# Neighbourhood attention beside a projection stream: value products of two steps in one visit, and three items of the recurrent branch moved in the written order

## The chip, the core and the metric

One core of a Trainium2 chip runs the whole layer. The metric is the device time of the program in microseconds, the median of several executions. TensorE (PE) does the matrix products, VectorE (DVE) and ScalarE (ACT) the elementwise work, GpSimd (POOL) some multiplies and memsets, and SyncE (SP) issues most of the DMAs. Each engine works through its own queue in order and waits for the others at semaphores.

## The reference, cut to what matters

The program is one layer of a hybrid model: 512 latent tokens on an 8 x 64 grid and 128 context tokens, 1024 features. One branch is a recurrent one (RWKV-7, two directions), the other an attention over a neighbourhood of the grid:

```python
def row_block(args):
    q_r, r0, dr = args
    k_r = lax.dynamic_slice_in_dim(kg, r0, kr, axis=1)[:, :, k_col]
    v_r = lax.dynamic_slice_in_dim(vg, r0, kr, axis=1)[:, :, k_col]
    ...
    lw = jnp.einsum("bjqhd,bkjchd->bhjqkc", q_r, k_r).astype(jnp.float32) * scale + bias[None]
    lw = jnp.where(valid[:, :, None, :], lw, NEG_INF)
    lc = jnp.einsum("bjqhd,blhd->bhjql", q_r, k_ctx).astype(jnp.float32) * scale
    logits = jnp.concatenate([lw.reshape(bsz, h, n_cb, NA_QCOLS, n_win), lc], axis=-1)
    p = jax.nn.softmax(logits, axis=-1).astype(v.dtype)
    ...
    return (jnp.einsum("bhjqkc,bkjchd->bjqhd", pw, v_r)
            + jnp.einsum("bhjql,blhd->bjqhd", pc, v_ctx))
```

Context tokens attend to all context tokens. Of the recurrent branch only the preparation matters here: per direction a decay that is summed along the sequence in blocks of 64, and the keys, normalised per head (`kk = kk * rsqrt(sum(kk * kk))`) and scaled by the decay.

## The kernel before

The grid is cut into four blocks of 16 columns, 128 queries each; the context tokens are a fifth block. Eight heads are four pairs (`ft`). So there are twenty items `k = 5 * ft + j`, with `j` from 0 to 3 for the column blocks and 4 for the context. The value of an item passes through these functions:

- `na_l(k)`: logits of the two heads into one PSUM tile `lg` (L942). For `j < 4` VectorE adds the mask and bias and takes the maximum (L948), for `j = 4` it only reduces (L955). It returns the exponentials, which ScalarE does (L952 or L957).
- `na_m(k)`: VectorE's reciprocals of the sums (L964), then GpSimd's multiply of the weights, one per head (L965).
- `na_t(k)`: TensorE transposes the weights (L971) into two PSUM tiles `pt`, ScalarE copies them to `PT` (L976).
- `na_o(k)`: TensorE multiplies with the values (L989) into one PSUM tile `po`, twelve matmuls for `j < 4`: two chunks of the window and one of the context, for two heads. `split` then writes the rounded part into `on` (ScalarE, L204) and the rest (VectorE, L205). At `j = 4` the two tiles `on` of the head pair are sent to memory (`o_d`, L996). `on` has one buffer of each kind, so the next head pair's first split waits until these have been sent.

These are not called item by item but in 22 steps, written out by hand in the table `na`. Step `k` does `na_o(k - 2)`, `na_l(k)`, `na_t(k - 1)`, the exponentials of `k`, then `a` units of the projection stream (`some(a)`: matmuls of L216 into tiles `mm`, with the elementwise work that falls due), `na_m(k)`, `p` items of the recurrent branch's preparation, `b` more units of the stream, `q` more items, and `n` pieces of the modulation product (`ada`, matmuls of L1027 into `psa`, whose weights arrive in tiles `wa` and `f`). A table entry is `a.p.b.q.n`. In this stretch the order of TensorE, VectorE, ScalarE and GpSimd is the written one.

The preparation is a generator, `prep_0`, and `next(pre0)` is one item. Counted in its order, items 9 and 10 are the five transposes of the key norm into the two `pt` tiles (L671) and the product that reads them and makes `kk` (L674, L676, VectorE). Items 11 and 12 are scale and scan of the first direction (L685, L688), 19 and 20 those of the second. Items 24 to 27 are four products of the first direction on VectorE (L710, L715, L721, L725). In the table before, 9 and 10 are at the end of step 13, 19 and 20 behind `na_m(17)`, 26 and 27 behind `na_m(19)`. After the 22 steps comes the recurrent scan, which begins with VectorE's products into `AG` (L1148).

## Time and profile before

| | us |
|---|---|
| median of 3 executions | 1171.59 (1171.57 to 1172.24) |
| profiled execution | 1170.39 |
| its span, first to last instruction | 1168.6 |
| TensorE busy in it | 1123.1 |
| VectorE busy | 775.6 |
| ScalarE busy | 535.4 |
| GpSimd busy | 194.3 |

The profile is of one execution; its span is a little shorter than the time of the execution, and that execution is a little shorter than the median. Busy time of TensorE counts its matmuls from start to modelled end, so a TensorE that is busy throughout is not at its peak. In the rows below, the first two numbers are start and length in us from the span's start, the count stands behind the x, and the brackets hold the idle time of the engine before the row and what ended it. The attention steps run from 121 to 256 us.

### The profile page before, as it was taken

The numbers are of one execution on the slowest core, as the hardware profiler recorded it, in microseconds if no ns is written. First come the engines' busy times: TensorE is split into PE (matmuls) and PEld (weight loads), VectorE is DVE, ScalarE is ACT, GpSimd is POOL, SyncE is SP. The second block draws the span as 40 slices with busy tenths as digits, with TensorE's granted clock in tenths as the row PEclk, the third lists the DMA queues.
The fourth block names the chain that finished last, engine by engine and source line by source line (L and its number), as shares of the span: only waits on it lengthen the run. The fifth ranks groups of instructions, "written<-read, shape, count | busy, mean of one in ns | idle before, by whom it ended". The sixth has DMA issues, their size and how long they took to land.

```text
span 1168.6 us, 26884 instructions
## 1 busy us (share of the span) xinstructions
PE 1123.1 (96%) x11160; PEld 995.0 (85%) x11160; DVE 775.6 (66%) x1639; ACT 535.4 (46%) x1054; POOL 194.3 (17%) x264
## 2 busy tenths in 40 slices
PE   6999999999999999999899899989999999999998
PEld 4688877789888988888788778989899989998997
DVE  4565365569558847945577856877567756875775
ACT  4444566554565665557353424644224423441330
POOL 1163244320101212110200241100000000001000
PEclk9999999999999999999999999999999999999999
DMA  9752777654433433343843772322212321232122
GB/s 338 259 117 81 229 245 226 200 145 117 110 85 88 133 82 91 105 107 91 276 130 108 239 217 67 96 73 85 97 54 91 100 87 67 73 108 90 54 83 98
DMA packets 60770, 150.21 MB, mean 129 GB/s; under 512 B 7492, under 2 KB 22468, under 8 KB 60648
## 3 DMA queue, kind: packets, MB, share of 16 engines
q1 hardware_dynamic: 55464, 131.56, 34.4%
q0 software_dynamic: 4320, 15.73, 6.9%
q8 instruction: 88, 1.44, 0.5%
q10 hardware_dynamic: 864, 1.20, 0.4%
q14 instruction: 34, 0.28, 0.1%
HBM read 118.41 MB, written 14.32 MB: 114 GB/s over the span
## 4 chain that ended last, share of the span: by engine, by line
PE 60%; DVE 7%; issue 7%; ACT 3%; DMA 1%; SPq 0%; POOL 0%; DVEq 0%; ACTq 0%; POOLq 0%
PE f L1814 23%; PE acc L303 16%; PE fl L216 10%; DVE pr L1293 1%; PE mm L216 1%; PE w L1394 1%; DVE RL L1297 1%; PE w L1367 1%; PE w L1191 1%; PE w L1407 1%; DMA o<-o_d 1%; PE w L1379 1%; PE w L1169 1%; ACT wlo L183 1%; PE w L1239 0%
## 5 line engine op out<-in xcount | busy, mean ns | idle before, releaser
L1814 PE MATMUL f<-t,whi 128*128 128x320 f32 x640 | 141.4, 309 | 0.0
L1814 PE MATMUL f<-b,whi 128*128 128x320 f32 x608 | 136.4, 312 | 3.6 <-ACT b L204 1.8
L303 PE MATMUL acc<-whi,u 128*128 128x512 f32 (+1 forms) x448 | 135.9, 385 | 0.0
L216 PE MATMUL fl<-h,whi 128*128 128x320 f32 x672 | 121.3, 320 | 0.8 <-issue 0.8
L1814 PEld LDWEIGHTS f<-t,whi 128*128 128x128 f32 x640 | 106.9, 188 | 0.0
L1814 PEld LDWEIGHTS f<-b,whi 128*128 128x128 f32 x608 | 102.7, 189 | 4.7 <-ACT b L204 2.2
L216 PEld LDWEIGHTS fl<-h,whi 128*128 128x128 f32 x672 | 101.5, 188 | 5.5 <-issue 0.9
L185 ACT CAST whi<-wst 128x1024 fp32r<-128x1024 f32 (+1 forms) x77 | 79.1, 1033 | 56.1 <-PE acc L303 42.5
L1814 PE MATMUL f<-t,wlo 128*128 128x320 f32 x320 | 98.9, 309 | 0.0
L303 PEld LDWEIGHTS acc<-whi,u 128*128 128x128 f32 x448 | 83.5, 188 | 16.6
L1814 PE MATMUL f<-b,wlo 128*128 128x320 f32 x304 | 94.6, 311 | 1.4 <-DVE wlo L1858 1.4
L1855 ACT CAST whi<-ws 128x1024 fp32r<-128x1024 f32 x40 | 42.0, 1050 | 108.4 <-PE f L1814 48.2
L303 PE MATMUL acc<-wlo,u 128*128 128x512 f32 (+1 forms) x224 | 86.3, 385 | 0.0
L1869 POOL TENSOR_TENSOR ws<-wst 128x512 f32<-128x512 f32 x20 | 28.0, 1402 | 341.3 <-DVE wlo L1858 247.7
L188 DVE TENSOR_TENSOR wlo<-wst,whi 128x1024 fp32r<-128x1024 f32 (+2 forms) x55 | 58.3, 1072 | 31.8 <-ACT whi L185 31.2
L303 PE MATMUL acc<-whi,h 128*128 128x512 f32 x240 | 78.5, 401 | 0.8 <-DVE h L428 0.8
L1691 DVE SCALAR_TENSOR_TENSOR tt<-acc,G 128x512 f32<-128x512 f32 (+1 forms) x51 | 34.7, 680 | 59.3 <-PE acc L303 45.3
L216 PE MATMUL fl<-h,wlo 128*128 128x320 f32 x336 | 63.5, 321 | 0.0
L1855 ACT CAST whi<-wst 128x1024 fp32r<-128x1024 f32 (+1 forms) x48 | 41.3, 868 | 42.3 <-PE acc L303 25.1
L1814 PEld LDWEIGHTS f<-t,wlo 128*128 128x128 f32 x320 | 60.1, 188 | 0.0
L1858 DVE TENSOR_TENSOR wlo<-ws,whi 128x1024 fp32r<-128x1024 f32 x40 | 55.0, 1374 | 6.3 <-ACT whi L1855 6.3
L1814 PEld LDWEIGHTS f<-b,wlo 128*128 128x128 f32 x304 | 57.6, 190 | 1.7 <-DVE wlo L1858 1.7
(342 smaller groups left out, 2512.8 us busy)
## 6 DMA issues: line engine op xcount, KB each, us to landing
wst<-in_w_dram SPq DMA_DIRECT2D x66, 512.0 KB
wst<-in_w_rw_dram SPq DMA_DIRECT2D x31, 512.0 KB
wlo<-wst POOLq DMA_DIRECT2D x30, 512.0 KB, 4.6
wa<-in_w_ada_dram SPq DMA_DIRECT2D x24, 512.0 KB
f<-in_w_ada_dram SPq DMA_DIRECT2D x16, 512.0 KB
wst<-in_w_qkv_dram SPq DMA_DIRECT2D x12, 512.0 KB
o<-o_d SPq DMA_DIRECT2D x14, 320.0 KB
x<-in_xs_dram SPq DMA_DIRECT2D x8, 512.0 KB
```

What stands on the lines that cost most here:

```text
L183: act.activation(lo[:, :n], st[:, :n], AF.Copy, scale=-1.0)
L185: act.copy(hi[:, :n], st[:, :n])
L188: dve.tensor_tensor(out=lo[:, a:b], in0=st[:, a:b], in1=hi[:, a:b].bitcast(F32), op=ALU.subtract)
L216: pe.matmul(ps[:, :t1 - t0], w[:, a:a + 128], x[:, k0 + kt, t0:t1], start=n == 0, stop=n == 3 * nk - 1)
L303: pe.matmul(pss[i][:, a:b], lhs(x, kt, ts_), w[:, cs_], start=ki == 0 and n == 0, stop=ki == last and n == 2)
L1169: pe.matmul(t[r0:r0 + 32, 64 * i:64 * i + 64], S.BK[l // 10][own, l % 10, 0, 32 * bk:32 * bk + 32], V(AG[own, l, h, :], [[0, 2], [1, 32]], ...
L1191: pe.matmul(pr[h][hrows[h ^ i], o_], x[hrows[h], :], R_[hrows[h], l, :], start=True, stop=True)
L1691: dve.scalar_tensor_tensor(out=tt, in0=ps[:, a:b], scalar=c, in1=G[:, g, sl], op0=ALU.mult, op1=ALU.mult)
L1814: pe.matmul(ps[:, :H2], w_[:, c_], x_[:, kt, :], start=first and kt + n == 0, stop=last and kt == 3 and n == 2, skip_group_check=more)
L1855: act.copy(r[0][:, :width], src())
L1858: dve.tensor_tensor(out=r[1][:, :width], in0=src(), in1=r[0][:, :width].bitcast(F32), op=ALU.subtract)
L1869: eng_x(PRM["se"][i - 1]).tensor_tensor(out=o_, in0=x, in1=y, op=op)
```

## The change

`na_o` takes a count. Items 0 and 1 of a head pair are multiplied in one visit (two sets of twelve matmuls, into columns 0 to 127 and 128 to 255 of one `po` tile), items 2 and 3 in another, item 4 alone; one split serves both items of a visit. The visits of the four head pairs are in steps 3, 5 and 6, 8, 10 and 11, 13, 15 and 16, 18, 20 and 21; steps 2, 4, 7, 9, 12, 14, 17 and 19 have none. Before, each of the steps 2 to 21 has one. The table entry gains a sixth number: items of the preparation that come before `na_m(k)`. With it and the old numbers, items 9 and 10 go from the end of step 13 to behind `na_m(14)`, items 19 and 20 from behind `na_m(17)` to ahead of it, and items 26 and 27 from behind `na_m(19)` to ahead of it.

```diff
-        "6.0.12.0.2 6.0.12.1.0 6.1.12.1.2 6.2.12.2.0 6.1.12.2.2 6.0.12.2.0 6.1.12.1.2 6.2.14.2.0 "
-        "6.2.14.1.2 6.2.14.2.0 6.2.14.2.0 6.3.18.2.0 10.0.10.0.0"))
+        "6.0.12.1.0 6.1.12.1.2 6.2.12.2.0 6.1.12.0.2 6.2.12.2.0 6.1.12.1.2 6.2.14.2.0 6.0.14.1.2.2 6.2.14.2.0 "
+        "6.0.14.2.0.2 6.3.18.2.0 10.0.10.0.0"))
...
-            def na_o(k):
+            def na_o(k, nb):
...
-                vts = (*vch[j], cvt) if j < 4 else (vpr,)
-                for c, vt in enumerate(vts):
-                    for hd in range(2):
-                        hc = (2 * ft + hd) * 64
-                        pe.matmul(pso[64 * hd:64 * hd + 64, :128], vt[:, hc:hc + 64],
-                                  blk[k][hd][:, c * 128:(c + 1) * 128], start=c == 0, stop=c == len(vts) - 1)
+                for i in range(nb):
+                    vts = (*vch[j + i], cvt) if j < 4 else (vpr,)
+                    for c, vt in enumerate(vts):
+                        for hd in range(2):
+                            hc = (2 * ft + hd) * 64
+                            pe.matmul(pso[64 * hd:64 * hd + 64, 128 * i:128 * i + 128], vt[:, hc:hc + 64],
+                                      blk[k + i][hd][:, c * 128:(c + 1) * 128], start=c == 0, stop=c == len(vts) - 1)
                 if j < 4:
-                    split(*(V(t[:, :], [[1, 16], [64, 8]], 16 * j) for t in on[ft]), V(pso[:, :], [[8, 16], [1, 8]]))
+                    split(*(V(t[:, :], [[16, 2], [1, 16], [64, 8]], 16 * j) for t in on[ft]),
+                          V(pso[:, :], [[128, 2], [8, 16], [1, 8]]))
...
-                    a, p, b, q, n = (int(x) for x in step.split("."))
-                    if 2 <= k < 22:
-                        na_o(k - 2)
+                    a, p, b, q, n, s_ = (int(x) for x in (step + ".0").split(".")[:6])
+                    ft, j = divmod(k - 3, 5)
+                    if ft < 0 or ft > 3:
+                        pass
+                    elif j == 0:
+                        na_o(5 * ft, 2)
+                    elif j == 2:
+                        na_o(5 * ft + 2, 2)
+                    elif j == 3:
+                        na_o(5 * ft + 4, 1)
...
                     some(a)
+                    for _ in range(s_):
+                        next(pre0, None)
                     if k < 20:
                         na_m(k)
```

More of the change, by code (lines that the diff above doesn't have):

```diff
@@ L74 @@
     wl="dddddddddppppppppppppppppppppppppppdddd", nu=9, lg=14, jo=(2, 0, 1), na=(
-        "6.0.12.0.1 6.0.12.0.0 6.0.12.0.0 6.0.12.0.2 6.0.12.0.0 6.0.12.0.2 6.0.12.0.0 6.0.12.0.2 6.0.12.0.0 "
-        "6.0.12.0.2 6.0.12.1.0 6.1.12.1.2 6.2.12.2.0 6.1.12.2.2 6.0.12.2.0 6.1.12.1.2 6.2.14.2.0 "
-        "6.2.14.1.2 6.2.14.2.0 6.2.14.2.0 6.3.18.2.0 10.0.10.0.0"))
+        "6.0.12.0.1 6.0.12.0.0 6.0.12.0.0 6.0.12.0.2 6.0.12.0.0 6.0.12.0.2 6.0.12.0.0 6.0.12.0.2 6.0.12.0.0 6.0.12.0.2 "
+        "6.0.12.1.0 6.1.12.1.2 6.2.12.2.0 6.1.12.0.2 6.2.12.2.0 6.1.12.1.2 6.2.14.2.0 6.0.14.1.2.2 6.2.14.2.0 "
+        "6.0.14.2.0.2 6.3.18.2.0 10.0.10.0.0"))
 MANUAL = {mybir.EngineType.PE}
```

## The prediction, made before the change was run

> **What bounds the kernel now.** I read the page first, then the table of stretches, then the rows of each engine in time order through the attention stage (121 to 256 us). From the page one line carries the argument: the chain that ended last is mostly TensorE's own work.

> ```profile
> PE 60%; DVE 7%; issue 7%; ACT 3%; DMA 1%; SPq 0%; POOL 0%; DVEq 0%; ACTq 0%; POOLq 0%
> ```

> So an edit that leaves TensorE's work alone can gain only what TensorE waits, or runs at a reduced clock. The table of stretches (time, then busy time of TensorE and its weight loads, VectorE, ScalarE, GpSimd, granted clock, DMA) shows where this stage loses both:

> ```profile
> 220.00:240.00 20.00, 18.00 (x141) 15.01 (x139) 11.17 (x26) 13.36 (x34) 6.96 (x8) 0.91 0.39 128
> ```

> Two microseconds idle and a clock of 0.91. TensorE's rows in order of time (start, length, count, and in brackets the idle time before and what ended it) give the places:

> ```profile
> 206.84 0.85 PE L971 MATMUL pt<-K,L 128*128 128x128 f32 x6 [0.97 <-DVE kk L674]
> ...
> 210.25 0.66 PE L989 MATMUL po<-PT,va 128*64 128x128 f32 x8
> 210.74 0.39 PE L989 MATMUL po<-PT,cvt 128*64 128x128 f32 x4
> 211.06 0.70 PE L942 MATMUL lg<-bv,q 64*128 64x256 f32 x4
> ...
> 232.45 0.55 PE L971 MATMUL pt<-K,L 128*128 128x128 f32 x3 [0.57 <-POOL L L965]
> 234.42 0.55 PE L971 MATMUL pt<-K,L 128*128 128x128 f32 x3 [1.42 <-POOL P L692]
> 234.72 2.26 PE L216 MATMUL mm<-h,wlo 128*128 128x320 f32 x8
> 236.78 2.65 PE L216 MATMUL mm<-h,whi 128*128 128x320 f32 x12
> ...
> 246.12 0.33 PE L971 MATMUL pt<-K,L 128*128 128x128 f32 x1 [0.61 <-POOL L L965]
> 246.21 1.42 PE L216 MATMUL mm<-h,whi 128*128 128x320 f32 x8
> 247.47 1.34 PE L216 MATMUL mm<-h,wlo 128*128 128x320 f32 x8
> ```

> Each wait is of the transposes of the softmax weights (L971). In step 14 (206.84) they want the two `pt` tiles that the key product L674 still reads. In step 18 (232.45, 234.42) and step 20 (246.12) they want GpSimd's multiply L965; the memset L692 named at 234.42 only stands behind that multiply in GpSimd's queue. After step 18's waits the clock is halved: eight matmuls take 2.26 against 1.34 at 247.47, and twelve take 2.65, where 1.97 would be due (eight of them last from 246.21 to 247.47, 0.16 each, so four more add 0.63 to 1.34). The loss is 0.92 + 0.68 = 1.6 us.

> What is behind step 18's wait is read from the rows of ScalarE, VectorE and GpSimd:

> ```profile
> 225.84 0.39 ACT L204 CAST on<-po 128x128 fp32r<-128x128 f32 x1 [2.18 <-DMA o_d<-on]
> ```

> ```profile
> 209.74 1.57 DVE L688 TENSOR_TENSOR_SCAN pre<-K,pre 128x640 f32<-128x640 f32 x1
> ...
> 226.94 0.55 DVE L948 CUSTOM_DVE_ANT_1 L<-lg,bm 128x384 f32<-128x384 f32 x1
> ...
> 231.11 0.22 DVE L964 RECIPROCAL m<-m 128x1 f32<-128x1 f32 x2
> 231.24 0.47 DVE L685 TENSOR_SCALAR pre<-pre 128x640 f32<-128x640 f32 x1
> 231.75 1.99 DVE L688 TENSOR_TENSOR_SCAN pre<-K,pre 128x640 f32<-128x640 f32 x1
> ...
> 244.42 0.16 DVE L964 RECIPROCAL m<-m 128x1 f32<-128x1 f32 x1 [0.53 <-ACT L L957]
> 244.77 0.16 DVE L964 RECIPROCAL m<-m 128x1 f32<-128x1 f32 x1 [0.19 <-ACT L L957]
> 244.96 0.85 DVE L721 SCALAR_TENSOR_TENSOR f<-NK,pre 128x640 f32<-128x640 f32 x1
> 245.73 1.02 DVE L725 TENSOR_TENSOR f<-NK,pre 128x640 f32<-128x640 f32 x1
> ```

> ```profile
> 141.73 1.61 POOL L965 TENSOR_TENSOR L<-L,m 128x384 f32<-128x384 f32 x2 [6.49 <-PE psa L1027]
> ...
> 231.44 2.93 POOL L965 TENSOR_TENSOR L<-L,m 128x384 f32<-128x384 f32 x2 [8.70 <-DVE m L964]
> ...
> 244.73 1.34 POOL L965 TENSOR_TENSOR L<-L,m 128x128 f32<-128x128 f32 x2 [5.76 <-DVE m L964]
> ```

> In step 17 ScalarE stands 2.18 us before the cast into `on`, because the one buffer of `on` is still being written out (it was sent in step 16). Behind that cast in ScalarE's queue are the copies of `PT` and the exponentials; VectorE's half of the split and the masking of the logits (226.94) come as late. So the reciprocals come at 231.11, and then the scan (1.99, alone 1.57 at 209.74) runs beside GpSimd's multiplies, which take 2.93 against 1.61 for the same pair at 141.73.

> **The change part by part.**

> *Visits of the value product.* A visit holds TensorE from 210.25 to 211.06, 0.81 us. The last four of its matmuls take 0.39, one takes 0.27, so a pair (the two heads lie side by side) follows the one before by 0.11; six pairs more in the same visit cost 0.65. Merging saves 0.15 us a time, eight times over the stage: 1.2 us, 0.9 of it by step 17 (six visits). The work is the same, only changes between kinds of matmul go.

> The split after a merged visit handles 256 columns, which the trace does not show. The nearest row is the split of one step:

> ```profile
> L204 ACT CAST on<-po x20: 243/380/393, 130.4 to 251.1; 128x128 fp32r<-128x128 f32 x20
> ```

> Two of them take 0.76; at the slope between the contiguous form (0.24) and the strided one (0.38) nothing says that the second half is free, so the bounds are 0.5 and 0.76. I take 0.6, which leaves the visit 0.2 longer than a single one on ScalarE and on VectorE. It hides except where VectorE is itself late, in step 18: +0.2 there.

> *The steps left without a visit.* In steps 2, 4, 7, 9, 12, 14, 17 and 19 the transposes come 0.81 us earlier after the last step's multiply. Where the multiply is only just done, TensorE now waits, and the saved time is lost:

> ```profile
> 142.80 1.15 PE L971 MATMUL pt<-K,L 128*128 128x128 f32 x6
> ...
> 165.68 1.05 PE L1027 MATMUL psa<-f,cs 128*32 128x512 f32 x4 [0.40 <-DMA f<-in_w_ada_dram]
> ```

> In step 4 the multiplies end at 143.34 (141.73 + 1.61); the six transposes start at 142.80 and are stretched to 1.15 already (0.85 unhindered, at 206.84), so coming 0.81 earlier gains nothing there. At 165.68 TensorE waits for a weight that lands when it lands; arriving earlier in step 7 by 0.81 only lengthens that wait. The other early steps I leave at between 0 and 0.5 in all. Together these take back between 0.8 and 1.6 us: I take 1.1, nearer the middle, as two losses are seen and the others are not.

> *The key product to step 14.* The five transposes (L671) and two products (L674, L676) go from the end of step 13 to behind the reciprocals of step 14. The `pt` tiles are then free for L971, and the wait of 0.97 goes. VectorE does the same work later by the two reductions and the reciprocals, in time that it now has since it no longer stands behind TensorE; no queue but VectorE's and TensorE's is passed, and none of the moved items issues a DMA. Price if that cover fails: the same 0.97 in step 15.

> So TensorE starts step 17 earlier by 0.9 + 1.0 - 1.1 = 0.8 us.

> *Step 17: no cast into `on`, scan ahead of the reciprocals.* The cast is now in step 18, when the write-out has landed. ScalarE loses its wait of 2.18, and the masking of the logits comes about 2.2 us earlier. The scale and the scan (0.47 and 1.57) go ahead of the reciprocals; queued behind them on VectorE are the reciprocals, behind these GpSimd's multiply, and TensorE waits for that. Relative to the chain before, the reciprocals thus come at 231.11 - 0.8 - 2.2 + 2.04 = 230.2, the multiplies end at about 232.0 (1.61 alone) against 234.37, and TensorE, which reaches the transposes some 0.9 earlier than now, waits about 1.0 in place of 2.0. That is half the idle that went before the halved clock at 234.72, and I take it that the clock stays: 1.6 us more. By its own work TensorE would then reach step 20's transposes 0.8 + 1.0 + 1.6 us earlier, and 0.3 for two more merged visits: 3.7 us, at 241.8 in place of 245.5 (246.12 less its wait).

> *Step 19: the products L721 and L725 ahead of the reciprocals.* VectorE's chain decides step 20: it runs from 226.94 without much slack to the reciprocal at 244.77. It is earlier by 0.8 and 2.2, then by 0.4 for the scan without GpSimd beside it, later by 0.2 for the wide split. The products, at 0.85 each without GpSimd beside them, delay the reciprocals by 1.70 less the idle 0.53 and 0.19 that they fill, 0.98; the multiplies, then undisturbed, should take about 0.3 less than 1.34. Net +0.6 or +0.7; at the rows' own durations +1.15.

> Sum: -0.8 - 2.2 - 0.4 + 0.2 + 0.6 = **-2.6 us** where TensorE resumes in step 20 (246.12 now, 243.5 then). It waits some 1.7 us there, against 0.61: the wait of step 18 partly moves to step 20. What follows is the same work. The next consumer of VectorE's chain has room:

> ```profile
> 252.25 3.37 DVE L1148 TENSOR_TENSOR AG<-kk,P 64x640 f32<-64x640 f32 x4
> ```

> ```profile
> 259.56 1.61 PE L1169 MATMUL w<-AG,f 64*32 64x64 f32 x139
> ```

> AG is done at 255.62, 3.9 us before TensorE wants it, so an earlier TensorE carries its gain on. The profiled execution took 1170.39 us (span 1168.6), the median of the runs is 1171.59: from the first, 1167.8; on the median's footing **1169.0 us**.

> **The rivals.**

> *The clock is halved in step 20 instead.* An idle of 0.57 + 1.42 was enough in step 18, and 1.7 may do in step 20. For it: the idle is nearly as long. Against it: it is shorter, and the waits at 206.84 (0.97) and 246.12 (0.61) left the clock alone, so the limit lies somewhere between 1 and 2 us. Price 1.6: 1170.6 us. [...]

> *GpSimd's multiply becomes the bound in the steps without a visit* (the slower side). If the transposes wait in all of them, each loses 0.81 and the merged visit still costs its 0.65. By step 17 that is six times +0.65 less 1.0 for the key product, +2.9 in place of -0.8; the sum turns from -2.6 to +1.1, and with the halved clock in step 20 to +2.7: 1174.3 us. It decides from the point where most of these multiplies end less than 0.8 us ahead of the transposes. For it: step 4. Against it: in steps 2, 7, 9 and 12 TensorE's rows name no wait for the multiply as it is.

> *The products of step 19 cost nothing*, because VectorE gets there with more slack than I give it. Then TensorE's own sum holds, 3.7 and the wait of 0.61 that goes too: -4.3, 1167.3 us.

> *The change does not do what it says*: merged visits save nothing and the key product's wait returns in step 15. Then 0.9 and 1.0 are lost, -0.7: 1170.9 us.

> **How the numbers follow.** Forecast 0.44; its own range is 1168.4 to 1170.0 (the products at 0.3 to 1.15, the early losses at 0.8 to 1.6), and a little over half of it, 0.25, lies beyond 0.2% (2.3 us, about what a measurement of this kernel can tell from no change). Free products 0.20, halved clock 0.13, no saving 0.03, multiply as the bound 0.20. So faster 0.25 + 0.20 = 0.45, the same 0.19 + 0.13 + 0.03 = 0.35, slower 0.20. The range for 8 in 10 reaches from the free products with the early losses at their low end and step 18's remaining wait of 1.0 gone as well, 1167.3 - 0.3 - 1.0 = 1166.0, to the slower rival, 1174.3.

> **What would show it.** Right: no wait on `o_d` before the cast in step 17; no wait on `kk` in step 14; in step 18 waits of about 1 us and matmuls at full speed after; a wait of about 1.7 us at step 20's transposes with GpSimd's L965 named; eight visits of 24 matmuls lasting 1.46 us; a stretch from 220 to 240 with clock 1.0. Wrong: bracketed waits on L965 in steps 7, 9 or 12; a second wait on `o_d`; a clock below 1 around step 20; or the stage ending 2.6 us earlier and the end of the program not.

## The result and the profile after

The kernel after took **1177.75 us** (median of 6 executions, 1174.62 to 1181.41), the kernel before beside it 1171.58 us: ratio **1.0054, 95% interval 1.0040 to 1.0068**. It is slower, by more than the 0.2% that can be told apart; 1169.0 was forecast, with 1174.3 as the upper end. The profiled execution of the kernel after took 1175.27 us, with a span of 1173.4 us against 1168.6.

And yet the attention stage gained where it was predicted to, and nearly as much. In the table of stretches TensorE is busier from 220 to 240 us and its clock stays up:

```profile
220.00:240.00 20.00, 19.22 (x156) 16.28 (x155) 11.95 (x28) 14.43 (x34) 5.97 (x8) 1.00 0.41 134
```

TensorE's rows in order of time (start, length, count, idle time before it in brackets): a merged visit from 229.09 to 230.55, the waits of step 18 and their matmuls, the wait of step 20.

```profile
229.09 0.66 PE L990 MATMUL po<-PT,va 128*64 128x128 f32 x8
229.57 0.39 PE L990 MATMUL po<-PT,cvt 128*64 128x128 f32 x4
229.79 0.61 PE L990 MATMUL po<-PT,vs 128*64 128x128 f32 x8
230.23 0.39 PE L990 MATMUL po<-PT,cvt 128*64 128x128 f32 x4
230.55 0.70 PE L942 MATMUL lg<-bv,q 64*128 64x256 f32 x4
...
232.01 0.55 PE L971 MATMUL pt<-K,L 128*128 128x128 f32 x3 [0.54 <-POOL L L965]
232.80 0.55 PE L971 MATMUL pt<-K,L 128*128 128x128 f32 x3 [0.23 <-POOL P L692]
234.36 1.92 PE L216 MATMUL mm<-h,whi 128*128 128x320 f32 x12
...
243.21 0.69 PE L971 MATMUL pt<-K,L 128*128 128x128 f32 x2 [1.30 <-POOL L L965]
```

ScalarE's cast into `on`, now in step 18, waits for nothing, where it waited 2.18 us for `o_d` in step 17 before:

```profile
231.31 0.59 ACT L204 CAST on<-po 128x256 fp32r<-128x256 f32 x1
```

VectorE's scan now stands ahead of the reciprocals and takes 1.49 us:

```profile
228.56 0.49 DVE L685 TENSOR_SCALAR pre<-pre 128x640 f32<-128x640 f32 x1
229.08 1.49 DVE L688 TENSOR_TENSOR_SCAN pre<-K,pre 128x640 f32<-128x640 f32 x1
230.49 0.20 DVE L964 RECIPROCAL m<-m 128x1 f32<-128x1 f32 x2
```

The time is lost directly behind the stage, in the first products of the recurrent scan (L1180, L1169 before). They begin 2.57 us earlier than before (256.99 against 259.56), and after 150 of 160 matmuls TensorE stands still:

```profile
256.99 1.72 PE L1180 MATMUL w<-AG,f 64*32 64x64 f32 x150
263.89 0.44 PE L1180 MATMUL w<-AG,f 64*32 64x64 f32 x10 [5.18 <-issue]
...
264.96 2.33 PE L216 MATMUL fl<-h,whi 128*128 128x320 f32 x8
...
270.11 1.44 PE L216 MATMUL fl<-h,whi 128*128 128x320 f32 x8
```

The rows of the kernel before at the same work:

```profile
262.38 0.42 PE L1169 MATMUL w<-AG,f 64*32 64x64 f32 x21 [1.21 <-issue]
...
263.13 1.33 PE L216 MATMUL fl<-h,whi 128*128 128x320 f32 x8
...
267.00 1.43 PE L216 MATMUL fl<-h,whi 128*128 128x320 f32 x8 [0.76 <-issue]
```

"issue" means that the profile shows nothing TensorE waited for. The gain of 2.57 us thereby becomes a loss of 1.40 at the same product (5.18 us of waiting in place of 1.21). Then its matmuls are slow: eight of L216 take 2.33 us against 1.33. The stretches of 2 us (busy time of TensorE, granted clock, DMA) show the clock halved up to about 269.7:

```profile
260.00:262.00 2.00, 0.00 (x0) 1.00 0.93 269
262.00:264.00 2.00, 0.11 (x6) 0.72 0.56 144
264.00:266.00 2.00, 2.00 (x16) 0.50 0.39 154
266.00:268.00 2.00, 2.00 (x33) 0.50 0.00 0
268.00:270.00 2.00, 2.00 (x80) 0.57 0.00 0
```

At the next common row the loss is 3.11 us (270.11 against 267.00). The slow clock thus cost about 2.5 us, an estimate from these rows: 3.11 less 1.40, and 0.76 more because only the kernel before waits ahead of that row. Later there are three more waits of the same kind, 3.2 us in all; before there was one of 0.3:

```profile
PE w L1202 <- issue: 3.2, 3, 2.1
```

At the end of the span the loss is 4.8 us, less than these sum up to, as TensorE waits less for other things on the way.

### The profile page after: what moved, and what is told of

The parts are those of the page before. It is cut to its first block, busy times and chain, and to the rows that moved or that the text cites. A ratio compares the mean times of both kernels' runs of the same rounds, so it can differ in the third digit from the quotient of the medians.

```text
span 1173.4 us, 26846 instructions
## 1 busy us (share of the span) xinstructions
PE 1124.7 (96%) x11160; PEld 997.0 (85%) x11160; DVE 772.3 (66%) x1631; ACT 534.6 (46%) x1046; POOL 191.8 (16%) x264
## 4 chain that ended last, share of the span: by engine, by line
PE 73%; DVE 10%; issue 8%; ACT 5%; DMA 2%; POOL 1%; SPq 1%; DVEq 0%; POOLq 0%; ACTq 0%
PE acc L303 23%; PE f L1825 21%; PE fl L216 10%; PE mm L216 4%; PE psa L1029 1%; PE pt L971 1%; PE po L990 1%; DVE pr L1304 1%; PE lg L942 1%; DVE RL L1308 1%; PE w L1202 1%; PE w L1405 1%; PE w L1378 1%; DVE wlo L188 1%; DMA f<-in_w_ada_dram 1%
## 5 line engine op out<-in xcount | busy, mean ns | idle before, releaser
L216 PE MATMUL fl<-h,whi 128*128 128x320 f32 x672 | 122.5, 322 | 0.0
L216 PEld LDWEIGHTS fl<-h,whi 128*128 128x128 f32 x672 | 102.6, 190 | 4.8
L216 PE MATMUL fl<-h,wlo 128*128 128x320 f32 x336 | 63.8, 322 | 0.0
```

The costliest lines, as they stand in the source:

```text
L216: pe.matmul(ps[:, :t1 - t0], w[:, a:a + 128], x[:, k0 + kt, t0:t1], start=n == 0, stop=n == 3 * nk - 1)
```

## The experiments

**The theory.** TensorE ran out of code. The page counts code as a DMA queue of its own:

```profile
q8 instruction: 88, 1.44, 0.5%
```

That is 16.4 KB a packet, and TensorE's 22486 recorded instructions in 88 packets make 256 in each. Counting its instructions in order of time from 0 (weight loads, matmuls and semaphore waits), the 5.18 us lie directly ahead of instruction 3777, and the 1.21 us of the kernel before lie ahead of instruction 3777 too, though this is another matmul. The change left out none of TensorE's matmuls ahead of the recurrent scan, but 23 of its semaphore waits (57 for 80). So the scan's first product is instruction 3477 where it was 3500, and the end of the code that TensorE holds comes 23 instructions later in the work. In the kernel before the next packet starts at 260.02 and TensorE resumes at 262.38, 2.36 us behind; in the kernel after it starts at 261.50 and TensorE resumes at 263.89, 2.39 us behind. TensorE is at instruction 3594 when the one starts; when the other starts, it has stood still since 258.71. In between GpSimd's accumulating transfer of a weight (L184, 512 KB on q0) takes 100.7% of the time of the 16 DMA engines from 258 to 260 us and 58.5% from 260 to 261.

**The rivals.** The recurrent products wait for something the profile does not show, a PSUM buffer or a semaphore; or the moved and paired work costs the time by itself.

The table gives every run. "At 110" and "at scan" say how far TensorE stands from the kernel before ahead of the attention steps (aligned by its instructions) and at the scan's first product; their difference is what the stage gained, since the start of the program varies by a microsecond or more. "Index" is the place of that product among TensorE's instructions (the expectations give places that are 35 lower, of a semaphore wait recorded ahead of it); "waits" are the idle times behind it that end at "issue", up to 275 us, and "later" is the sum of those after that. The runs were made in several sessions, in which the kernel before had medians of 1170.8 to 1171.6 us; the ratio is to that of the same session, so kernels are compared by the ratio.

| kernel | index | at 110 | at scan | waits | later | us | ratio to before (95%) |
|---|---|---|---|---|---|---|---|
| before | 3500 | 0 | 0 | 1.2, 0.8 | 0.3 | 1171.6 | 1 |
| after | 3477 | +0.3 | -2.6 | 5.2 | 3.2 | 1177.75 | 1.0054 (1.0040 to 1.0068) |
| a_pad24 | 3521 | -1.0 | -4.2 | 1.3, 1.2 | 0.3 | 1169.37 | 0.9979 (0.9969 to 0.9989) |
| a_pad48 | 3569 | 0.0 | -3.1 | 1.9 | 5.2 | 1181.27 | 1.0088 (1.0071 to 1.0104) |
| a_nodma | 3477 | 0.0 | -2.8 | 3.9 | 3.1 | 1174.37 | 1.0021 (1.0009 to 1.0033) |
| b_less24 | 3452 | -0.4 | -0.8 | 5.2 | 2.2 | 1180.76 | 1.0076 (1.0057 to 1.0095) |
| a_pad22 | 3501 | +0.7 | -2.4 | 0.9, 1.0 | 1.0 | 1169.68 | 0.9982 (0.9971 to 0.9993) |
| pair_only | 3479 | +0.3 | +0.9 | 2.2 | 2.6 | 1174.86 | 1.0031 (1.0018 to 1.0044) |
| move_only | 3500 | -0.1 | -1.5 | 0.5, 1.0 | 0.7 | 1169.73 | 0.9987 (0.9978 to 0.9997) |
| a_pad24_nodma | 3521 | -0.8 | -5.1 | 0.8, 0.9 | 1.1 | 1168.75 | 0.9979 (0.9965 to 0.9993) |
| b_pad20 | 3517 | +1.1 | +1.1 | 0.9, 1.4 | 0.3 | 1171.64 | 1.0008 (0.9997 to 1.0019) |
| b_nodma | 3500 | -0.8 | -0.4 | 0.7, 0.5 | 1.1 | 1170.12 | 0.9996 (0.9987 to 1.0005) |
| pair_pad22 | 3503 | -0.6 | -0.8 | 1.1, 0.8 | 0.6 | 1171.27 | 1.0009 (0.9998 to 1.0020) |
| a_pad22_nodma | 3501 | +0.3 | -1.6 | 0.6, 0.5 | 0.8 | 1169.33 | 0.9982 (0.9972 to 0.9992) |

In the traces of all fourteen kernels, every wait of these two columns lies ahead of an instruction 3777 + 256 n. In the kernel after the places are 3777, 7617, 10945 and 14273.

### a_pad24: more TensorE instructions ahead of the scan

```diff
                 pso = pp.tile([P, 512], F32, tag="po", bufs=1, name=nm("po"))
+                for _ in range(1):
+                    pe.matmul(pso[:64, 256:272], ident[:, :64], ident[:, :16], start=True, stop=True)
                 for i in range(nb):
```

> The kernel after with one tiny matmul (64x16, its result is never read) ahead of each of the twelve value visits: 12 weight loads and 12 matmuls, 24 more TensorE instructions ahead of the first recurrent products, on places where TensorE waits anyway. Theory (TensorE ran out of code: its code comes in packets of 256 instructions, the change made its stream 23 instructions shorter ahead of these products, so the packet was asked for that much later in the work, when the accumulate transfer of the weights was running): the idle time inside the recurrent products goes from 5.18 us to 1 to 2 us, the clock is not halved behind it, the gain of the attention stage shows, and the time is 1169 to 1171 us. Rival (the products wait for something that the profile does not show, a PSUM buffer or a semaphore): the 5.2 us stay and the time is 1176 to 1178.5 us.

1169.37 us, faster than both kernels: the 5.18 us are 1.30, and the halved clock is gone (its eight matmuls of L216 take 1.33 again). TensorE's rows:

```profile
255.35 1.48 PE L1182 MATMUL w<-AG,f 64*32 64x64 f32 x128
258.13 0.46 PE L1182 MATMUL w<-AG,f 64*32 64x64 f32 x32 [1.30 <-issue]
...
258.93 1.33 PE L216 MATMUL fl<-h,whi 128*128 128x320 f32 x8
```

The wait now comes after 128 of the products, not 150, but still ahead of instruction 3777. A hidden dependency of the products would not move like that. The 4.2 us at the scan don't last: in this trace 0.5 are left at the end of the program. One number of the expectation was wrong: each tiny matmul of this type shows as two weight loads and two matmuls, so 48 instructions were added, and 4 waits went: 44 in all.

### a_pad48: twice as many

The same edit with `range(2)`.

> The same with two tiny matmuls ahead of each value visit: 48 more TensorE instructions. Code theory: the packet is asked for another 24 instructions earlier in the work, so the idle time is 0 to 1 us, and the time is 1168.5 to 1171 us, unless the tiny matmuls themselves cost some tenths each. Rival (hidden dependency): 5.2 us of idle time stay, 1176 to 1179 us.

1181.27 us: slower, a miss. At instruction 3777 there is no wait any more, as expected. But the later edges are moved as well, and TensorE now waits at other places (L1204's wait is at 263.41, ahead of instruction 4033, which is 3777 + 256; the others are ahead of 5057, 7105 and 15041):

```profile
PE w L1201 <- issue: 2.0, 1, 2.0
PE w L1204 <- issue: 1.9, 1, 1.9
PE fl L216 <- issue: 1.8, 1, 1.8
PE w L1182 <- issue: 1.4, 1, 1.4
```

7.1 us in four places. They are not the whole loss: between 560 and 620 us TensorE also waits 7.0 us for tiles `o` from memory, where the kernel before waits 3.1, and the granted clock is 0.89 on average there, against 0.97. Why these transfers come later against the work is open.

```profile
PE fl L216 <- DMA o<-o_d: 7.0, 7, 2.8
```

More instructions are thus not better as such; it counts where the edges fall.

### a_nodma: no accumulating transfer beside the packet

```diff
-    wl="dddddddddppppppppppppppppppppppppppdddd"
+    wl="dddddddddpdppppppppppppppppppppppppdddd"
```

> The kernel after, with the one weight that is cast at 254 us split on VectorE instead of by GpSimd's accumulating transfer, so that no such transfer runs when the code packet is asked for. TensorE's instructions stay what they are. Code theory, if the accumulating transfer is what the code packet stands behind: the packet starts 2 to 4 us earlier than 261.5, the idle time falls from 5.2 to 1 to 3 us, the clock stays up, and the time is 1169.5 to 1173 us. If the packet is late for its own reasons (asked for late, the other transfers of that time): 4 to 5.2 us stay and the time is 1175 to 1178.5 us.

1174.37 us, the wait 3.90 us: between the two expectations.

```profile
262.41 0.44 PE L1180 MATMUL w<-AG,f 64*32 64x64 f32 x10 [3.90 <-issue]
```

The packet starts at 259.84 in place of 261.50. So the transfer is a part of the delay, 1.3 of 5.2 us, and not all of it. The median fell by more, 3.4 us, which the trace doesn't explain: its execution took 1176.51 us, 2.1 above the median of this kernel. In the kernel after its queue takes all 16 DMA engines from 258 to 259 us (packets, MB, share of the engines' time):

```profile
q0 software_dynamic: 45, 0.18, 100.7%
```

Without it the other queue does, in the same microsecond:

```profile
q1 hardware_dynamic: 201, 0.37, 108.8%
```

That the packet stands behind whatever fills the engines fits both lines; when it is asked for, no view shows.

### b_less24: the kernel before, with fewer instructions

```diff
-                vts = (*vch[j], cvt) if j < 4 else (vpr,)
+                vts = ((*vch[j], cvt)[:2 if k < 7 else 3]) if j < 4 else (vpr,)
```

> The kernel before, with the third product (the one with the common chunk) left out of the six early blocks 0, 1, 2, 3, 5 and 6: 12 matmuls and 12 weight loads less ahead of the recurrent products, so TensorE's stream there is as short as in the kernel after, and nothing of the change is in it. Code theory: the packet comes as late against the work as in the kernel after, the idle time grows from 1.2 to about 5 us, the clock is halved behind it, and the time is 1174.5 to 1179 us, though this kernel does less work. Rival (the loss comes from the moved or paired work): the idle time stays 1.2 us and the time is 1170.5 to 1172 us.

1180.76 us (four executions), 0.8% slower than the kernel before with less work and nothing of the change, and above the expected range. The wait of 5.22 us is there, ahead of instruction 3777, which is now a projection matmul behind the recurrent products:

```profile
258.75 1.82 PE L1169 MATMUL w<-AG,f 64*32 64x64 f32 x160
260.50 0.56 PE L216 MATMUL fl<-h,wlo 128*128 128x320 f32 x2
260.90 0.31 PE L216 MATMUL fl<-h,whi 128*128 128x320 f32 x1
266.42 2.23 PE L216 MATMUL fl<-h,whi 128*128 128x320 f32 x7 [5.22 <-issue]
```

The 160 products run through. So the wait needs neither a hidden dependency of the products nor the moved work: it falls where the count of instructions puts it, whatever the operation. (48 instructions were left out, not 24; so the edge lies further on than in the kernel after.)

### a_pad22: the edges where they were before

```diff
+                if j == 2 or j == 0 and ft < 2:
+                    pe.matmul(pso[:64, 256:272], ident[:, :64], ident[:, :16], start=True, stop=True)
```

> The kernel after with the tiny matmul ahead of six of the twelve value visits only. Each such matmul showed as four TensorE instructions in the runs so far (two weight loads, two matmuls), not two as the earlier expectation said: this kernel's first recurrent product is the 3466th recorded TensorE instruction, where it was the 3465th before and the 3442nd after. All later block edges fall on the same instructions as before, within one. Code theory: every wait for code behind the stage is as before (1.2 us in the first recurrent products, under 1 us each later), the whole stage gain of 2.5 us stays up to the end unless the clock is halved in another place, 1168 to 1170.5 us. Rival (a hidden dependency that the 48 instructions of the first kernel broke by chance, or the later waits belong to the change): 3 to 5 us idle stay, 1174 to 1178 us.

1169.68 us, ratio 0.9982: with the edges on the old instructions the change is a gain, 0.18%. TensorE comes to the products as early as in the kernel after, so coming early is not what costs the 5.18 us by itself. Its rows:

```profile
257.20 1.61 PE L1182 MATMUL w<-AG,f 64*32 64x64 f32 x138
259.75 0.42 PE L1182 MATMUL w<-AG,f 64*32 64x64 f32 x22 [0.94 <-issue]
```

TensorE is 2.36 us ahead at 257.20, 2.0 at 590 and 3.0 at 668 us. In the profiled execution most of this goes between 668 and 676 us, in two waits for VectorE's `tr` where the kernel before has one of 0.4. The same two waits stand in the traces of b_pad20, which has nothing of the change, a_pad24_nodma and a_pad22_nodma, and in no other; what causes them is open.

```profile
PE fl L1665 <- DVE tr L1666: 2.5, 2, 1.6
```

### pair_only and move_only: the parts alone

The table string of the kernel before in the kernel after, and the other way round (with the sixth number).

> The kernel after with the table of the kernel before: value products in pairs, no key product or scan moved. The stream ahead of the recurrent products keeps nearly all of the lost instructions (about 22 fewer than before). Code theory: 4 to 5.5 us idle in the first recurrent products and a halved clock behind it, 1175 to 1179 us, whatever the stage gains (0.5 to 2.2 us from the wait for o_d that goes). Rival (the moves cost it): idle 1.2 us and 1170 to 1172 us.

> The kernel before with the table of the kernel after: key product and scan of the second direction moved, value products one block a visit as before. TensorE's stream ahead of the recurrent products is as long as before. Code theory: idle 1 to 1.5 us there, the stage ends 0.5 to 1.5 us earlier (the wait for kk of 1.0 us goes, step 17 keeps its o wait), 1169.5 to 1171.5 us. Rival (the moves cost the time): 1174 to 1178 us.

Pairs alone: 1174.86 us, just under the expected range. The wait in the first products is 2.21 us, less than expected, with the clock not halved behind it (its eight matmuls of L216 take 1.33), and a second of 2.2 us follows later. The edge lies within two instructions of the kernel after's, yet the wait is less than half as long: the count says where TensorE waits, and how long depends on when the packet comes (here at about 262.0, as TensorE runs dry at 262.19: an estimate, 264.40 less the 2.4 us from packet to resumption in the kernels before and after). The stage itself gained nothing; the wait for `kk` has grown from 0.97 to 1.78:

```profile
207.92 0.84 PE L971 MATMUL pt<-K,L 128*128 128x128 f32 x6 [1.78 <-DVE kk L674]
264.40 0.33 PE L1180 MATMUL w<-AG,f 64*32 64x64 f32 x11 [2.21 <-issue]
```

Moves alone: 1169.73 us, ratio 0.9987, in the expected range. The code edges stay (index 3500), the stage ends 1.5 us earlier and the wait is 0.47, less than the 1 to 1.5 expected:

```profile
258.03 1.61 PE L1171 MATMUL w<-AG,f 64*32 64x64 f32 x139
260.12 0.42 PE L1171 MATMUL w<-AG,f 64*32 64x64 f32 x21 [0.47 <-issue]
```

So it is the pairing that takes the semaphore waits out of TensorE's stream: ahead of the first product the kernel with pairs has 59 of them, the one with the moves 80 as before.

### a_pad24_nodma: both cures

> The kernel after with the tiny matmul ahead of all twelve visits and the weight cast at 254 us split on VectorE, so without the accumulating transfer beside the code packet. Code theory: packet as early against the work as in the run with the twelve tiny matmuls, and 1 to 2 us less in front of it: idle 0 to 1 us in the first recurrent products, 1167 to 1169.5 us. If the transfer matters only where the packet is late: the same as with the twelve tiny matmuls alone, 1169 to 1170 us.

1168.75 us, ratio 0.9979: the lowest median, but by its interval not to be told from a_pad24. The wait is 0.75 us against 1.30. The transfer lengthens the wait in every pair of kernels, by 0.3 to 0.6 us where the packet is early and 1.3 where it is late; a change of the time clear of the noise is seen in the last case alone.

### The controls: b_pad20, b_nodma, pair_pad22, a_pad22_nodma

b_pad20 has the tiny matmul in the kernel before under `if j == 2 or k == 0:`; the other three combine edits shown above.

> The kernel before with the tiny matmul ahead of five of its twenty value visits: its stream ahead of the recurrent products is some 17 to 20 instructions longer, about where the kernel after with twelve tiny matmuls stands. Nothing of the change is in it. If part of that kernel's gain is the place of the code edges and not the change: idle 1 to 1.5 us at the edge as there, 1170 to 1172 us, and the change by itself is then worth the distance, 1 to 3 us. If the tiny matmuls alone make the gain (by the clock or by the code): 1168 to 1169.5 us.

> The kernel before with the one weight that is cast at 257 us split on VectorE instead of by GpSimd's accumulating transfer: the control for the kernels that have this with the change. Idle at the edge 0.5 to 1.2 us (1.2 before), 1169.5 to 1171.5 us. If the transfer is all that the code packet stands behind, the idle time is gone and it gains 1 us or more; if it does not matter where the packet is early, no change.

> Pairs alone (the table of the kernel before) with the tiny matmul ahead of six of the twelve visits, so that the block edges fall on the instructions of the kernel before. Code theory: the two waits for code of 2.2 us are back at 1 us or less each, and what pairing by itself is worth shows: the stage ends 0.5 us earlier to 1 us later than before (the wait for kk stays and was 1.8 us with pairs), 1169.5 to 1172.5 us. If pairing costs by itself: 1174 us or more as without the tiny matmuls.

> The kernel after with the tiny matmul ahead of six visits and the weight cast at 254 us split on VectorE. Both cures together: idle at the edge 0 to 0.9 us, stage end 2.4 us earlier than before as with the six alone, 1167.5 to 1169.7 us. If the transfer does not matter once the packet is early: 1169 to 1170 us as with the six alone.

The tiny matmuls by themselves bring nothing (1.0008, interval with 1 in it), nor does the cast on VectorE by itself (0.9996). Against b_pad20, whose edges lie within four instructions of a_pad24's, the change is worth 0.9979 / 1.0008 = 0.9971, 3.4 us (some 1.7 to 5 by the two intervals, an estimate). Pairs alone on the old edges: 1.0009, the stage 0.2 us shorter, the later wait of 2.2 us gone as well:

```profile
258.78 1.56 PE L1182 MATMUL w<-AG,f 64*32 64x64 f32 x137
261.43 0.42 PE L1182 MATMUL w<-AG,f 64*32 64x64 f32 x23 [1.09 <-issue]
```

So in the stage neither half makes the gain: it is shorter by 0.2 us with pairs (0.6 longer in pair_only), 1.4 with the moves, and some 3 with both (after, a_pad22; 1.9 to 4.3 over the seven kernels with both). The time doesn't show this: the moves alone make 0.9987, both on the old edges 0.9982, and the intervals overlap. a_pad22_nodma gains what a_pad22 does (0.9982 both): its shorter waits are not seen in the time.

## Why the prediction was wrong

**The step that failed** is the last one of the sum: "What follows is the same work", and the room for `AG`, from which it has "an earlier TensorE" carry its gain on. In the trace 2.57 us of gain at the scan became 4.8 us of loss at the end. The work is the same, its code's place is not. The prediction counted the operations of TensorE and not its semaphore waits, though the trace has each of them as an instruction in its stream (23 fewer, and the scan's first product is 3477 where it was 3500); it did not read the line of q8, and it did not ask what the "1.21 <-issue" of the first recurrent products was, which is seen in the trace before. Its own list of signs has the case, "the stage ending 2.6 us earlier and the end of the program not", but no rival stood behind it and no price: the slower rival was another one.

**The steps of the stage held in the main.**

- *Visits*: 1.46 us for a merged visit as worked out (229.09 to 230.55). The wide split takes 0.59 on ScalarE, 0.6 had been taken:

```profile
243.71 0.59 ACT L204 CAST on<-po 128x256 fp32r<-128x256 f32 x1
```

- *Steps without a visit*: the two losses are where they were put, in steps 4 and 7, 0.79 us (0.55 and 0.24) and 0.7 (0.68 and 0.42 against 0.40 before), with 0.2 at 193.03: 1.7 us for 1.1, a little over the upper bound of 1.6. The wait at 193.03 is in step 12, where the prediction called one a sign of being wrong; it is small. A wait of 0.34 in step 5 of the kernel before (148.84) is gone, which the prediction didn't count.

```profile
142.76 0.55 PE L971 MATMUL pt<-K,L 128*128 128x128 f32 x3 [0.55 <-POOL L L965]
143.54 0.55 PE L971 MATMUL pt<-K,L 128*128 128x128 f32 x3 [0.24 <-POOL L L965]
164.54 1.05 PE L1029 MATMUL psa<-wa,cs 128*32 128x512 f32 x4 [0.68 <-DMA wa<-in_w_ada_dram]
166.02 1.05 PE L1029 MATMUL psa<-f,cs 128*32 128x512 f32 x4 [0.42 <-DMA f<-in_w_ada_dram]
193.03 0.55 PE L971 MATMUL pt<-K,L 128*128 128x128 f32 x3 [0.20 <-POOL L L965]
```

- *Key product*: TensorE's waits in the stage name `kk` no more, as forecast.
- *Step 17*: reciprocals at 230.49 where 230.2 was worked out; waits of 0.77 in step 18 (0.54 and 0.23) for 1.0; the twelve matmuls behind take 1.92 and not 2.65, the clock stays. That it stays is luck in part. The prediction put the limit between 1 and 2 us of waiting, but with the moves alone TensorE waits 2.54 and 0.24 us at this place, and eight matmuls behind it still take 1.42:

```profile
232.76 0.55 PE L971 MATMUL pt<-K,L 128*128 128x128 f32 x3 [2.54 <-POOL L L965]
...
233.85 1.42 PE L216 MATMUL mm<-h,wlo 128*128 128x320 f32 x8
```

- *Step 20*: TensorE comes at 241.91 (243.21 less 1.30) for 241.8, waits 1.30 for 1.7, resumes at 243.21 for 243.5. The rival of a clock halved by that wait did not come.
- *The sum*: 2.91 us where TensorE resumes in step 20 (243.21 for 246.12) and 2.57 at the scan's first product, forecast 2.6. That it fits so closely is luck in part: the losses of the early steps were 0.6 larger than forecast and the waits in steps 18 and 20 smaller by 0.2 and 0.4, and in the seven kernels with both parts the stage gains between 1.9 and 4.3. With the edges of the code put back (a_pad22) the time is 0.18% below the kernel before, 2.1 us (0.8 to 3.4 by the interval) of the 2.6 that were forecast.

So the mechanism in the stage was right in place and nearly in size, and the forecast of the whole was wrong in sign: by the table TensorE waits 8.4 us for code where it waited 2.3, and with some 2.5 us for the halved clock this outweighs 2.57.

**What stays open**: at which instruction a packet is asked for, and in which order the DMA engines serve it, and so what sets the length of a wait; and when idle time halves the clock. The median of the kernel after is 2.5 us above its profiled execution; where the others lose that, no trace shows.

## What to carry to other kernels

In these runs an edit that changed how many instructions TensorE executes, semaphore waits among them, moved every later edge of its code. Before a small change is called good or bad, look for idle time ended by "issue" and count instructions up to it. If it always comes at the same count, put the old count back with a few idle instructions where the engine waits anyway, and compare then. The dangerous place here was a run of very short matmuls with large transfers beside it.
